# Expert weights in pairs of places, router logits with tokens on partitions, and a later second gather

## The chip, the cores and the metric

One core of a Trainium2 chip runs the whole program. The metric is device time in microseconds (us) of one execution; the number given for a kernel is the median of its runs. A span is the time from the first to the last instruction of a profiled execution.

## The reference

A batch of one sequence of 256 tokens with 1024 features passes a first transformer block and then two layers of a second block; everything is float32. A layer of the second block is

```python
h = h + hybrid_mixer(rmsnorm_2(h, norm_mix[l]), ...)       # two attentions, gates, output projection
h = h + expert_choice_ffn(rmsnorm_2(h, norm_ffn[l]), ...)
```

and the expert part is

```python
cap = CAPACITY_FACTOR * S // N_EXPERTS                      # 2 * 256 / 16 = 32 tokens for each expert
aff = softmax(einsum('bsd,de->bse', h, w_router), axis=-1)  # 256 tokens x 16 experts
gate, idx = top_k(swapaxes(aff, 1, 2), cap)                 # each expert picks its 32 tokens
xe = h[bidx, idx]
a = einsum('becd,edf->becf', xe, w_gate)
u = einsum('becd,edf->becf', xe, w_up)
ye = einsum('becf,efd->becd', silu(a) * u, w_down)
out = zeros_like(h).at[bidx, idx].add(gate[..., None] * ye)
```

All 16 experts run with three matrices of 1024 x 1024 each, so a layer reads 192 MB of expert weights.

## The kernel before

**Program.** `first_block()` runs once; then, for each of two layers, `mixer` and `experts`. The order of the instructions on each engine is chosen by a scheduler that simulates a timeline: of the instructions that are ready it takes the one that stands first in the source. On the chip every engine keeps that order.

**Weights of the experts.** They are stored as 192 chunks a layer (`NCHUNK`), each 128 partitions of 2048 floats: 1 MB in rows of 8 KB. `Experts.load` brings the next chunk to the next place of a fixed cycle: one place "q" (the tile Qb), NA0 = 4 places "a0", NA = 6 places "a1", "Ha" and "Hb" (the two halves of the activations' pair), NB = 1 place "b", RING = 3 places "r" (the ring that also holds the mixer's weights), NSPLIT = 4 places "s" (the buffers of the split mixer weights). The first time round two places "x" follow (parts of W, and XB). That is 21 places, and 23 for the first round. A chunk's DMA is issued on SP's queue and waits there until its place is free. Each DMA also has one of eight semaphores in turn, so a ninth is issued when the first of eight has landed.

**Loading ahead.** While the mixer runs, `prefetch` and `pace` issue the first chunks behind the mixer's own loads: "q" and four "a0" between the query projections, six "a1" between the gate projections (`pace`), "Ha" and "Hb" at the sixth merge, then "b" when the gates' pool closes. The places "r" and "s" come free one by one as the output projection ends, W when the last merged activations M are used up, XB when the tokens' features xg have been transposed (L1133).

**End of the mixer.** The output projection makes eight tiles (`out_tiles`), each of 24 matmuls (L141 to L143) on split weights. After tile k, DVE adds it to x and forms xg[k] = x[k] * gain (L979, L980); ACT squares x[k]. For k = 7 the order is another: xg[7] is finished first (L983, L984), then x[7] (L985), then its square (L987). The router's logits are summed by matmuls with the router's 32 padded columns of feature block k as weights and xg[k], 256 tokens, as moving columns (L994): experts on partitions, four blocks side by side in four groups of 32 partitions; half of them after tile 3, half after tile 7. Then ACT copies the sums (L999), and two matmuls with a constant "sum4" (L1009) add the four groups and turn the result to tokens on partitions. In between, the mean square is summed (L1003) and its root taken by ACT (L201). The logits are scaled by 1/rms (L1014), their maximum is taken off (L1101, L1102), and ACT makes the exponentials (L1103), for which it loads another table.

**Experts.** Each of the four groups of four experts takes 16 chunks for the gate matrices (bank G), 16 for up (U), 16 for down (E), a chunk for eight matmul instructions (L1190). The inputs of the experts are gathered by `gather(k0)`: matmuls with a selection matrix (L1205) and a copy by ACT (L1209), feature block by feature block. `grouped` calls the gather of the next block through `ahead` before the matmuls of each chunk:

```python
for k0 in range(0, KT, kn):
    for b in banks:
        w = xl.take()
        if ahead:
            ahead(k0 + 1)
```

So gather(0) and gather(1) come before the first chunk's matmuls. In the first group the scheduler puts chunks of U between those of G where a gather is waited for. The last 16 chunks of a layer are issued one behind the other, and the last of all as two halves of 4 KB rows.

Of the kernel before, what the change touches and what calls it, by code (L numbers as in the profile page):

```python
# [10 lines left out]
F32 = mybir.dt.float32  # L11
# [27 lines left out]
PV, NPV = _places([("final_g", 8), ("norm_mix", 16), ("b_gate", 32), ("norm_ffn", 16), ("router", 512)])  # L39
# [5 lines left out]
CV, NCV = _places([("ident", 128), ("ones_d", 1), ("ones_h", 1), ("slot", 32), ("sum4", 16)])  # L45
# [8 lines left out]
RING, NA0, NA, NB, NSPLIT = 3, 4, 6, 1, 4  # L54

ENDS = ((0, 512), (512, 256), (768, 256))

SCRATCH = 2048
# [3 lines left out]
def tile_net(ctx: ExitStack, tc: tile.TileContext, a, out):  # L62
# [109 lines left out]
    def act_pair():  # L172
        return tuple(hp.tile([P, KT, T], F32R, name=f"H{c}", tag=f"H{c}") for c in "ab")
# [530 lines left out]
    def mixer(l, h, stats, w0=None):  # L704

        with ExitStack() as es:
# [17 lines left out]
            xl.r2a.append(late.enter_context(tc.tile_pool(name=f"e{l}a0", bufs=NA0, side="right", reuse_waits="tile")))  # L724
# [143 lines left out]
            xl.prefetch(1, True)  # L868
# [51 lines left out]
            xl.r2a.append(late.enter_context(tc.tile_pool(name=f"e{l}a", bufs=NA, side="right", reuse_waits="tile")))  # L920
# [47 lines left out]
            xl.r2b = late.enter_context(tc.tile_pool(name=f"e{l}b", bufs=NB, reuse_waits="tile"))  # L968
            xl.prefetch(NB)
# [3 lines left out]
            at = PV["router"][0] + 256 * l  # L973
# [24 lines left out]
            lp = cp.tile([P, T], F32, name="lp", tag="sq", bufs=2)  # L998
            nc.scalar.copy(lp, pl[:, :T])  # L999
            ms = psv()  # L1000
            for t in range(2):
                for i, s in enumerate((acc, sq7)):
                    nc.tensor.matmul(  # L1003
                        ms[:, t : t + 1], s[:, t * P : t * P + P], con("ones_d"), start=i == 0, stop=i == 1
                    )
# [8 lines left out]
            nc.vector.tensor_tensor(  # L1014
                lg, pls[:, 0:32].rearrange("p (t e) -> p t e", t=2), by_expert(rt), op=ALU.mult
            )
# [7 lines left out]
    class Experts:  # L1024


        def __init__(self, l):
            self.l, self.r2a, self.r2b, self.at, self.dma = l, [], None, 0, None
            self.have, self.n, self.wait = [], 0, 4

            self.cycle = ["q"] + ["a0"] * NA0 + ["a1"] * NA + ["Ha", "Hb"] + ["b"] * NB + ["r"] * RING + ["s"] * NSPLIT
            self.places = self.cycle + ["x", "x"]

        def load(self, paced=False):
            i = len(self.have)
            end = i >= NCHUNK - sum(cn for _, cn in ENDS) * KT // 512
            while True:
                where = self.places.pop(0)
                if not self.places:
                    self.places = list(self.cycle)  # L1040

                if not (end and where in ("Ha", "Hb")):
                    break
# [4 lines left out]
            else:  # L1048
                pool, tag = {
                    "q": (qp, "Qb"), "a0": (self.r2a[0], "w2"), "a1": (self.r2a[-1], "w2"), "b": (self.r2b, "w3"),  # L1050
                    "r": (ring, "w"), "Ha": (hp, "Ha"), "Hb": (hp, "Hb"),
                }[where]
                t = pool.tile([P, CH], F32, name="we", tag=tag)
# [3 lines left out]
            src = a["w_exp"][self.l, i]  # L1057

            for c0, cn in ((0, 1024), (1024, 1024)) if i == NCHUNK - 1 else ((0, CH),):
# [3 lines left out]
            self.have.append(t)  # L1063
# [420 lines left out]
```

## Time and profile before

| | |
|---|---|
| median of 3 runs | 1884.87 us (1884.21 to 1887.2) |
| profiled execution | 1885.2 us, of which span 1883.3 us |
| TensorE busy | 1594.7 us, 85% of the span |
| VectorE busy | 825.0 us, 44% |
| ScalarE busy | 628.9 us, 33% |
| chain that ended last | 53% PE, 44% DMA; 42% DMA of expert weights alone |
| moved by DMA | 562.49 MB, mean 299 GB/s |

The shares are means over stages that differ: in the mixers TensorE is busy all the time and the DMA engines are not, in the experts it is the other way round. The chain that ended last says so in its two large shares.

### The profile page before, as it was taken

Reading aid. Unit: us, or ns where it says so; the run is one execution under the profiler, and the core shown is the slowest. Engines: PE = TensorE matmul, PEld = TensorE weight load, DVE = VectorE, ACT = ScalarE, POOL = GpSimd, SP = SyncE. Lnnn points to the kernel's source line nnn. Section 1 sums busy time; section 2 is a strip of 40 time slices with the busy share of each in tenths; the row PEclk is TensorE's granted clock in tenths of the full one; section 3 lists DMA queues with packets and bytes.
Section 4 is the critical chain, followed back from the end, with each engine's and each line's share of the span. In section 5 each row is a group of like instructions: output and inputs, shape, how many; then the busy total and the mean of one; then the engine's idle time right before and its main releaser. Section 6 shows DMA issues by size and latency. Waiting matters only on the chain.

```text
span 1883.3 us, 27589 instructions
## 1 busy us (share of the span) xinstructions
PE 1594.7 (85%) x11434; PEld 1076.1 (57%) x11434; DVE 825.0 (44%) x1481; ACT 628.9 (33%) x1130; POOL 41.2 (2%) x72
## 2 busy tenths in 40 slices
PE   8999999999999998876777667899998866766765
PEld 7899999999998897220211102888995211101101
DVE  8678777996687666100010001687573110000001
ACT  5566646665566543100000001566542100000001
POOL 0100000000011000000000000010000000000000
PEclk9999999999999999886777767999999877868768
DMA  7454455555562387999999999833487999999997
GB/s 250 169 191 165 171 191 179 179 181 185 217 241 90 114 328 274 402 420 420 419 420 420 420 420 419 340 136 112 181 321 307 419 420 420 419 420 419 420 420 309
DMA packets 83829, 562.49 MB, mean 299 GB/s; under 512 B 9452, under 2 KB 14456, under 8 KB 16888
## 3 DMA queue, kind: packets, MB, share of 16 engines
q1 hardware_dynamic: 83544, 560.20, 75.3%
q8 instruction: 90, 1.47, 0.3%
q10 hardware_dynamic: 160, 0.52, 0.1%
q14 instruction: 35, 0.29, 0.0%
HBM read 558.84 MB, written 1.85 MB: 298 GB/s over the span
## 4 chain that ended last, share of the span: by engine, by line
PE 53%; DMA 44%; DVE 1%; ACT 1%; issue 0%; SPq 0%; POOL 0%; ACTq 0%
DMA we<-in_w_exp_dram 42%; PE ps_d L141 14%; PE ps_d L142 14%; PE ps_d L143 14%; PE ps_t L268 2%; PE ps_v L856 1%; PE ps_g L1190 1%; DMA w<-in_w_in_dram 1%; PE ps_u L1190 1%; PE ps_s L782 1%; PE ps_s L888 1%; PE ps_s L783 1%; PE ps_t L1205 0%; PE ps_s L385 0%; PE ps_v L906 0%; PE ps_v L912 0%
## 5 line engine op out<-in xcount | busy, mean ns | idle before, releaser
L141 PE MATMUL ps_d<-Ha,ws 128*128 128x256 f32 x1408 | 403.6, 287 | 9.4 <-ACT Ha L188 7.7
L143 PE MATMUL ps_d<-Ha,ws 128*128 128x256 f32 x1408 | 403.3, 286 | 1.2 <-DVE ws L136 1.2
L142 PE MATMUL ps_d<-Hb,ws 128*128 128x256 f32 x1408 | 402.4, 286 | 0.2 <-DVE Hb L189 0.2
L136 DVE TENSOR_TENSOR ws<-w,ws 128x1024 fp32r<-128x1024 f32 x282 | 344.3, 1223 | 122.7 <-ACT ws L135 119.6
L135 ACT CAST ws<-w 128x1024 fp32r<-128x1024 f32 x282 | 294.3, 1047 | 277.2 <-PE ps_d L143 248.3
L141 PEld LDWEIGHTS ps_d<-Ha,ws 128*128 128x128 f32 x1408 | 271.9, 193 | 12.7 <-ACT Ha L188 7.7
L143 PEld LDWEIGHTS ps_d<-Ha,ws 128*128 128x128 f32 x1408 | 271.6, 193 | 4.0 <-DVE ws L136 1.8
L142 PEld LDWEIGHTS ps_d<-Hb,ws 128*128 128x128 f32 x1408 | 271.7, 193 | 2.9 <-issue 1.2
L1190 PE MATMUL ps_u<-we,W 128*32 128x512 f32 x992 | 189.0, 840 | 91.5 <-DMA we<-in_w_exp_dram 91.5
L1190 PE MATMUL ps_g<-we,W 128*32 128x512 f32 x1024 | 175.5, 782 | 74.2 <-DMA we<-in_w_exp_dram 74.2
L1190 PE MATMUL ps_e<-we,W 128*32 128x512 f32 (+1 forms) x1152 | 163.2, 671 | 61.7 <-DMA we<-in_w_exp_dram 61.6
L1190 PEld LDWEIGHTS ps_u<-we,W 128*32 128x32 f32 x992 | 25.2, 125 | 241.0 <-DMA we<-in_w_exp_dram 225.8
L1190 PEld LDWEIGHTS ps_g<-we,W 128*32 128x32 f32 x1024 | 26.4, 122 | 208.1 <-DMA we<-in_w_exp_dram 168.9
L1264 ACT ACTIVATE W<-ps_g 128x512 f32<-128x512 f32 x16 | 9.6, 597 | 380.9 <-PE ps_g L1190 380.9
L1190 PEld LDWEIGHTS ps_e<-we,W 128*32 128x32 f32 x1152 | 29.3, 118 | 163.9 <-DMA we<-in_w_exp_dram 124.0
L1266 DVE SCALAR_TENSOR_TENSOR W<-W,ps_u 128x512 f32<-128x512 f32 x16 | 11.0, 688 | 250.9 <-PE ps_u L1190 250.9
L1219 DVE COPY W<-ps_e 128x512 f32<-128x512 f32 (+1 forms) x18 | 11.4, 632 | 220.7 <-PE ps_e L1190 220.7
L1271 ACT COPY W<-ps_t 128x512 f32<-128x512 f32 x16 | 9.4, 586 | 278.4 <-PE ps_t L1270 278.4
L1265 DVE SCALAR_TENSOR_TENSOR W<-W,ps_g 128x512 f32<-128x512 f32 x16 | 11.0, 688 | 208.2 <-ACT W L1264 208.2
L141 PE MATMUL ps_d<-Y,ws 128*128 128x256 f32 x288 | 80.8, 281 | 0.0
L142 PE MATMUL ps_d<-Y,ws 128*128 128x256 f32 x288 | 80.7, 280 | 0.0
L143 PE MATMUL ps_d<-Y,ws 128*128 128x256 f32 x288 | 80.7, 280 | 0.0
(327 smaller groups left out, 2362.6 us busy)
## 6 DMA issues: line engine op xcount, KB each, us to landing
we<-in_w_exp_dram SPq DMA_DIRECT2D x378, 1024.0 KB, 19.9
w<-in_w_in_dram SPq DMA_DIRECT2D x46, 1024.0 KB, 4.9
w<-in_w_up_dram SPq DMA_DIRECT2D x22, 1024.0 KB, 4.8
w<-in_w_br_dram SPq DMA_DIRECT2D x18, 1024.0 KB, 4.8
w<-in_w_gate_dram SPq DMA_DIRECT2D x12, 1024.0 KB, 4.9
w<-in_w_out_dram SPq DMA_DIRECT2D x12, 1024.0 KB, 4.9
w<-in_w_down_dram SPq DMA_DIRECT2D x11, 1024.0 KB, 4.8
w<-in_w_rnn_dram SPq DMA_DIRECT2D x8, 1024.0 KB, 4.8
```

The source lines that it names most:

```text
L135: nc.scalar.copy(ws[:, 0], s)
L136: nc.vector.tensor_tensor(ws[:, 1], s, ws[:, 0].bitcast(F32), op=ALU.subtract)
L141: nc.tensor.matmul(ps, wh, xh, start=first, stop=False)
L142: nc.tensor.matmul(ps, wh, xl, start=False, stop=False)
L143: nc.tensor.matmul(ps, wl, xh, start=False, stop=last)
L268: nc.tensor.transpose(ps[:, i * P : i * P + P], b, ident)
L782: nc.tensor.matmul(ps, q, kh, start=True, stop=False)
L783: nc.tensor.matmul(ps, q, kl, start=False, stop=True)
L856: nc.tensor.matmul(po[64 * c : 64 * c + 64, :T], vw[:, k, kvh * 64 : kvh * 64 + 64], pts[c][:, k * T : k * T + T], start=k == 0, stop=k == 1,)
L888: nc.tensor.matmul(ps[:, o], qa[b, i, tk], ka[b, i, kr], start=True, stop=True)
L1190: nc.tensor.matmul(b[32 * e : 32 * e + 32, :cn], lhs[:, k, 32 * e : 32 * e + 32], cols(w, ((k - k0) * 4 + e) * cn, cn), start=k == 0, stop ...
L1219: nc.vector.tensor_copy(ye[:, s], E[:, :cn])
```

## The change

- Places "a0", "a1", "H" and "b" are joined in pairs: one tile of 128 x 4096 floats, one DMA of 2 MB, the weights packed in the host's array so that a pair has rows of 16 KB. "q", "r", "s", "x" and the last four chunks of a layer stay single. `_plan()` writes the order of places out ahead.
- NB goes from 1 to 2, so the cycle has 22 places and the first round 24. The padding of the router's weights and "sum4" go, and the DMA scratch is halved.
- `prefetch` and `pace` ask half as often for pairs: three times for "q" and "a0" between the query projections instead of five, every second time in `pace`.
- The router's logits are made with xg[k] as weights (128 tokens at a time) and the router's 16 columns as moving operand, two matmuls after each tile; the sum over k is in the accumulation, so L999 and L1009 go. The maximum is taken off before the scaling by 1/rms.
- For k = 7 the order is that of the other tiles: x[7], then xg[7].
- The sums of squares are taken block by block, so that those of `acc` come before those of the last square.
- `ahead` isn't called for the first chunk: gather(1) comes behind the first chunk's matmuls.

```diff
-RING, NA0, NA, NB, NSPLIT = 3, 4, 6, 1, 4
+RING, NA0, NA, NB, NSPLIT = 3, 4, 6, 2, 4
...
+LAST = sum(cn for _, cn in ENDS) * KT // 512
-SCRATCH = 2048
+SCRATCH = 1024
+def _plan():
+    cycle = [("q", 1)] + [("a0", 2)] * (NA0 // 2) + [("a1", 2)] * (NA // 2) + [("H", 2)] + [("b", 2)] * (NB // 2)
+    cycle += [("r", 1)] * RING + [("s", 1)] * NSPLIT
+    places, plan, i = cycle + [("x", 1)] * 2, [], 0
+    while i < NCHUNK:
+        where, n = places.pop(0)
+        places = places or list(cycle)
+        if where == "H" and i + n > NCHUNK - LAST:
+            continue
+        n = n if i < NCHUNK - 4 else 1
+        plan.append((i, n, where))
+        i += n
+    return plan
...
     def act_pair():
-        return tuple(hp.tile([P, KT, T], F32R, name=f"H{c}", tag=f"H{c}") for c in "ab")
+        H = hp.tile([P, 2, KT, T], F32R, name="H", tag="H")
+        return H[:, 0], H[:, 1]
...
                 parts_q(qws[i], load(w1[l, 2 + i]))
-                xl.prefetch(1, True)
+                if i != 2:
+                    xl.prefetch(1, True)
...
             parts_q(qa0, load(w1[l, 6]))
-            xl.prefetch(1, True)
...
-                    xl.prefetch(2, True)
+                    xl.prefetch(1, True)
...
-            xl.prefetch(NB)
+            xl.prefetch(NB // 2)
...
+                    nc.vector.tensor_tensor(x[:, k, :], ps, x[:, k, :], op=ALU.add)
+                    nc.vector.tensor_scalar(xg[:, k, :], x[:, k, :], gain, None, op0=ALU.mult)
                     if k < KT - 1:
-                        nc.vector.tensor_tensor(x[:, k, :], ps, x[:, k, :], op=ALU.add)
-                        nc.vector.tensor_scalar(xg[:, k, :], x[:, k, :], gain, None, op0=ALU.mult)
                         square_in(acc, x[:, k, :], k == 0)
                     else:
-                        nc.vector.tensor_scalar(xg[:, k, :], x[:, k, :], gain, None, op0=ALU.mult)
-                        nc.vector.scalar_tensor_tensor(xg[:, k, :], ps, gain, xg[:, k, :], op0=ALU.mult, op1=ALU.add)
-                        nc.vector.tensor_tensor(x[:, k, :], ps, x[:, k, :], op=ALU.add)
                         sq7 = cp.tile([P, T], F32, name="sq7", tag="sq", bufs=2)
                         nc.scalar.activation(sq7, x[:, k, :], AF.Square)
+                    for t in range(2):
+                        nc.tensor.matmul(
+                            pl[:, 16 * t : 16 * t + 16], xg[:, k, t * P : t * P + P],
+                            pv[:, at + 16 * k : at + 16 * k + 16], start=k + t == 0, stop=k + t == KT,
+                        )
...
-                if j % 2 == 1:
-                    for k in range(2 * j - 2, 2 * j + 2):
-                        o = 32 * (k % 4)
-                        nc.tensor.matmul(
-                            pl[o : o + 32, :T], pv[:, at + 32 * k : at + 32 * k + 32], xg[:, k, :],
-                            start=j == 1, stop=j == 3,
-                        )
-            lp = cp.tile([P, T], F32, name="lp", tag="sq", bufs=2)
-            nc.scalar.copy(lp, pl[:, :T])
...
-            for t in range(2):
-                for i, s in enumerate((acc, sq7)):
+            for i, s in enumerate((acc, sq7)):
+                for t in range(2):
...
-            pls = pss()
-            for t in range(2):
-                nc.tensor.matmul(
-                    pls[:, 16 * t : 16 * t + 16], lp[:, t * P : t * P + P], con("sum4"), start=True, stop=True
-                )
...
+            nc.vector.tensor_reduce(mx, pl, axis=AX.X, op=ALU.max, negate=True)
+            nc.vector.tensor_tensor(lg, pl, by_expert(mx), op=ALU.add)
...
-            src = a["w_exp"][self.l, i]
+            src = a["w_exp"][self.l, i * P * CH : (i + m) * P * CH].rearrange("(p c) -> p c", p=P)
...
-            self.have.append(t)
+            self.have += [t[:, CH * j : CH * j + CH] for j in range(m)]
...
-            self.wait -= 1
-            if self.wait < 0 and len(self.have) < 1 + NA0 + NA:
+            self.asked += 1
+            if self.asked > 4 and self.asked % 2 and len(self.have) < 1 + NA0 + NA:
                 self.load(True)
...
-            nc.vector.tensor_reduce(mx, lg, axis=AX.X, op=ALU.max, negate=True)
-            nc.vector.tensor_tensor(lg, lg, by_expert(mx), op=ALU.add)
+            nc.vector.tensor_tensor(lg, lg, by_expert(rt), op=ALU.mult)
...
-                        if ahead:
+                        if ahead and (k0 > 0 or b is not banks[0]):
                             ahead(k0 + 1)
```

## Rows read from the trace of the kernel before

**Rows 1.** The page's slices of the span (40 of 47 us each), GB/s moved.
```profile
GB/s 250 169 191 165 171 191 179 179 181 185 217 241 90 114 328 274 402 420 420 419 420 420 420 420 419 340 136 112 181 321 307 419 420 420 419 420 419 420 420 309
```

**Rows 2.** Windows: us, busy time of each engine, granted clock, DMA share, GB/s.
```profile
720.00:760.00 40.00, 33.08 (x250) 24.28 (x253) 18.80 (x48) 12.41 (x24) 0.00 (x0) 0.91 0.68 260
...
760.00:1150.00 390.00, 278.09 (x1578) 63.08 (x1570) 27.02 (x44) 16.34 (x35) 0.00 (x0) 0.75 1.01 420
...
1400.00:1420.00 20.00, 20.00 (x159) 18.37 (x157) 12.62 (x25) 7.26 (x11) 0.00 (x0) 1.00 0.73 269
...
1435.30:1444.40 9.10, 6.96 (x40) 3.21 (x40) 2.46 (x6) 0.53 (x2) 0.00 (x0) 0.62 0.13 32
...
1500.00:1850.00 350.00, 236.64 (x1268) 42.32 (x1260) 20.71 (x30) 10.40 (x22) 0.00 (x0) 0.75 1.01 420
```

**Rows 3.** The page's DMA issues: count, size of each, us from issue to landing.
```profile
we<-in_w_exp_dram SPq DMA_DIRECT2D x378, 1024.0 KB, 19.9
w<-in_w_in_dram SPq DMA_DIRECT2D x46, 1024.0 KB, 4.9
```

**Rows 4.** Timeline of PE at the end of layer 0's experts: start, us, instruction.
```profile
1176.04 1.07 PE L1190 MATMUL ps_e<-we,W 128*32 128x256 f32 x16 [1.69 <-DMA we<-in_w_exp_dram]
1178.54 1.07 PE L1190 MATMUL ps_e<-we,W 128*32 128x256 f32 x16 [1.43 <-DMA we<-in_w_exp_dram]
...
1181.08 0.64 PE L1190 MATMUL ps_e<-we,W 128*32 128x256 f32 x8 [0.61 <-DMA we<-in_w_exp_dram]
```

**Rows 5.** Timeline of SP's queue at the end of layer 1's mixer.
```profile
1400.10 25.57 SPq L1062 DMA_DIRECT2D we<-in_w_exp_dram  x8
...
1442.17 7.81 SPq L1062 DMA_DIRECT2D we<-in_w_exp_dram  x7
```

**Rows 6.** Timeline of PE round a group of the router's matmuls in the output projection.
```profile
1411.31 0.28 PE L143 MATMUL ps_d<-M,ws 128*128 128x256 f32 x1
1411.52 0.62 PE L994 MATMUL ps_s<-xg,pv 128*32 128x256 f32 x4
...
1412.30 0.28 PE L142 MATMUL ps_d<-M,ws 128*128 128x256 f32 x1
```

**Rows 7.** Timeline of PE where another dense stream is cut by four small matmuls.
```profile
1193.63 0.28 PE L143 MATMUL ps_d<-Ha,ws 128*128 128x256 f32 x1
1193.75 0.50 PE L195 MATMUL ps_v<-cv,acc 128*128 128x1 f32 x4
...
1194.31 0.28 PE L143 MATMUL ps_d<-ws,Hb 128*128 128x256 f32 x1
```

**Rows 8.** Weight loads of two lines: ns min/median/max of one.
```profile
L994 PEld LDWEIGHTS ps_s<-xg,pv x32: 106/108/109, 723.8 to 1426.2; 128*32 128x32 f32 x32
...
L1003 PEld LDWEIGHTS ps_v<-cv,acc x8: 186/190/192, 738.0 to 1427.1; 128*128 128x128 f32 x8
```

**Rows 9.** Timeline of DVE in the output projection.
```profile
1410.37 1.22 DVE L136 TENSOR_TENSOR ws<-w,ws 128x1024 fp32r<-128x1024 f32 x1
1411.50 0.35 DVE L980 TENSOR_SCALAR xg<-x,pv 128x256 f32<-128x256 f32 x1
```

**Rows 10.** Timeline of DVE, PE and ACT from the last tile to the exponentials.
```profile
1425.36 0.48 DVE L984 SCALAR_TENSOR_TENSOR xg<-ps_d,pv,xg 128x256 f32<-128x256 f32 x1 [1.48 <-PE ps_d L143]
...
1427.42 0.60 PE L1009 MATMUL ps_s<-cv,lp 128*128 128x16 f32 x4
1427.60 0.26 ACT L201 ACTIVATE rtok<-ps_v,eps 128x2 f32<-128x2 f32 x1 [0.40 <-PE ps_v L1003]
...
1427.88 1.28 ACT L1103 ACT_TABLE_LOAD   x1
...
1429.17 0.23 ACT L1103 ACTIVATE lg<-lg 128x32 f32<-128x32 f32 x1
```

**Rows 11.** Timeline of PE at the second gather and the first chunk of layer 1.
```profile
1439.02 1.23 PE L1205 MATMUL ps_t<-sl,ht 128*128 128x128 f32 x4 [0.35 <-ACT W L1209]
...
1440.17 3.08 PE L1190 MATMUL ps_g<-we,W 128*32 128x512 f32 x16
```

More of the change, by code (lines that the diff above doesn't have):

```diff
@@ L723, in mixer @@
             xl = Experts(l)
-            xl.r2a.append(late.enter_context(tc.tile_pool(name=f"e{l}a0", bufs=NA0, side="right", reuse_waits="tile")))
+            xl.r2a.append(late.enter_context(tc.tile_pool(name=f"e{l}a0", bufs=NA0 // 2, side="right", reuse_waits="tile")))
             att = es.enter_context(ExitStack())
@@ L919, in mixer @@
             att.close()
-            xl.r2a.append(late.enter_context(tc.tile_pool(name=f"e{l}a", bufs=NA, side="right", reuse_waits="tile")))
+            xl.r2a.append(late.enter_context(tc.tile_pool(name=f"e{l}a", bufs=NA // 2, side="right", reuse_waits="tile")))
             M = qp.tile([P, 2, KT, T], F32R, name="M", tag="Qa")
@@ L967, in mixer @@
             bp = late.enter_context(tc.tile_pool(name=f"e{l}h", bufs=1, reuse_waits="tile"))
-            xl.r2b = late.enter_context(tc.tile_pool(name=f"e{l}b", bufs=NB, reuse_waits="tile"))
-            xl.prefetch(NB)
+            xl.r2b = late.enter_context(tc.tile_pool(name=f"e{l}b", bufs=NB // 2, reuse_waits="tile"))
+            xl.prefetch(NB // 2)
             acc = new_acc()
             xg = bp.tile([P, KT, T], F32, name="xg", tag="xg")
-            at = PV["router"][0] + 256 * l
+            at = PV["router"][0] + 128 * l
             pl = pss()
@@ L999, in mixer @@
-            nc.scalar.copy(lp, pl[:, :T])
             ms = psv()
-            for t in range(2):
-                for i, s in enumerate((acc, sq7)):
+            for i, s in enumerate((acc, sq7)):
+                for t in range(2):
                     nc.tensor.matmul(
-                        ms[:, t : t + 1], s[:, t * P : t * P + P], con("ones_d"), start=i == 0, stop=i == 1
+                        ms[:, t : t + 1], s[:, t * P : t * P + P], con("ones_d"), start=i + t == 0, stop=i + t == 2
@@ L1028, in __init__ @@
             self.l, self.r2a, self.r2b, self.at, self.dma = l, [], None, 0, None
-            self.have, self.n, self.wait = [], 0, 4
-            self.cycle = ["q"] + ["a0"] * NA0 + ["a1"] * NA + ["Ha", "Hb"] + ["b"] * NB + ["r"] * RING + ["s"] * NSPLIT
-            self.places = self.cycle + ["x", "x"]
+            self.have, self.n, self.plan, self.asked = [], 0, _plan(), 0
         def load(self, paced=False):
[L1035 to L1043, printed above, removed]
+            i, m, where = self.plan.pop(0)
+            end = i >= NCHUNK - LAST
             if where == "x":
@@ L1050, in load @@
                     "q": (qp, "Qb"), "a0": (self.r2a[0], "w2"), "a1": (self.r2a[-1], "w2"), "b": (self.r2b, "w3"),
-                    "r": (ring, "w"), "Ha": (hp, "Ha"), "Hb": (hp, "Hb"),
+                    "r": (ring, "w"), "H": (hp, "H"),
                 }[where]
-                t = pool.tile([P, CH], F32, name="we", tag=tag)
+                size = 2 * CH if where in ("a0", "a1", "H", "b") else CH
+                t = pool.tile([P, size], F32, name="we", tag=tag)
             if paced:
                 nc.gpsimd.tensor_copy(t[:, 0:1], turn[0][:, 0:1].bitcast(F32))
-            src = a["w_exp"][self.l, i]
-            for c0, cn in ((0, 1024), (1024, 1024)) if i == NCHUNK - 1 else ((0, CH),):
+            src = a["w_exp"][self.l, i * P * CH : (i + m) * P * CH].rearrange("(p c) -> p c", p=P)
+            for c0, cn in ((0, 1024), (1024, 1024)) if i == NCHUNK - 1 else ((0, m * CH),):
                 behind = self.dma if end else turn[1] if paced else None
@@ L1097, in bank @@
                 return pp.tile([P, 512], F32, name=f"ps_{tag}", tag=tag, bufs=bufs)
-            mx, sm, m8 = small("rmx", P, 2), small("rsm", P, 2), small("m8", 16, 8)
-            nc.vector.tensor_reduce(mx, lg, axis=AX.X, op=ALU.max, negate=True)
-            nc.vector.tensor_tensor(lg, lg, by_expert(mx), op=ALU.add)
+            sm, m8 = small("rsm", P, 2), small("m8", 16, 8)
+            nc.vector.tensor_tensor(lg, lg, by_expert(rt), op=ALU.mult)
             nc.scalar.activation(lg, lg, AF.Exp)
@@ L1281, in experts @@
                         if not last and c0 + cn == D:
-                            xl.prefetch(NCHUNK - len(xl.have))
+                            xl.prefetch(len(xl.plan))
                             with tc.issue_after(xl.dma.ins):
@@ L1343, in _experts @@
                 chunks.append(w.reshape(4, KT, P, 2, 512).transpose(1, 3, 2, 0, 4).reshape(-1, P, CH))
-    return np.concatenate(chunks, 0)
+    chunks = np.concatenate(chunks, 0)
+    return np.concatenate([chunks[i : i + n].transpose(1, 0, 2).reshape(-1) for i, n, _ in _plan()])
 def _cols(v):
@@ L1361, in _constants @@
     _put(c, CV, "slot", np.broadcast_to(np.arange(1, 33), (P, 32)))
-    _put(c, CV, "sum4", np.tile(np.eye(32, 16), (4, 1)))
     pos = np.arange(T)
@@ L1423, in _pack @@
     put("w_f", fl.reshape(8, P, 8).transpose(1, 0, 2).reshape(P, 64))
-    put("router", np.pad(i["w_router_2"].reshape(2, 8, P, 16).transpose(2, 0, 1, 3), ((0, 0), (0, 0), (0, 0), (0, 16))).reshape(P, 512))
+    put("router", i["w_router_2"].reshape(2, 8, P, 16).transpose(2, 0, 1, 3).reshape(P, 256))
     r["cv"], cmask, oh, r["far"] = _constants()
```

9 lines of the change are left out of this document (4 added, 5 removed).

## The prediction

> **What bounds the kernel now.** I read the slices of the page first. In them the reader is to see two kinds of stage: long stretches at about 420 GB/s, which are the experts of the two layers, and between them stretches at 90 to 330, which are the first block and the mixers [rows 1]. The windows put names to both: in 760 to 1150 and in 1500 to 1850 the DMA engines are busy all the time (share 1.01) while TensorE has about 70% at a mean granted clock of 0.75; in 1400 to 1420, the end of a mixer, TensorE is busy for all of the 20 us and the DMA share is 0.73 [rows 2]. So in the experts a us of TensorE is worth nothing and a MB is worth its transfer; in the mixers it is the reverse. A chunk of 1024 KB at 420 GB/s takes 2.50 us. The issues agree: a chunk lands 19.9 us after its issue, the time of eight, since eight are under way at once, while a mixer's load of the same size, with little in front of it, lands in 4.9, of which 2.5 are transfer and 2.4 lead [rows 3].
>
> Between the two kinds lies the piece that the change is about. SP's queue issues eight chunks from 1400.10 on as places come free, and the next one at 1442.17, when the first chunk has been used [rows 5]. In between all places are full: in 1435.3 to 1444.4 the DMA share is 0.13 [rows 2]. The end of a layer is therefore: the moment when the first chunk is used, 2.4 us of lead, and one transfer after the other for all chunks that were not loaded ahead, 192 less 23. Three things can move it: chunks loaded ahead, the time for a MB, and that moment.
>
> **One more place.** The round before the restart holds 24 chunks in place of 23, if the DMA engines have room for the 24th. They do: it is issued with the other "b" at 1400.10, and 1400 to 1420 leaves them 0.27 of 20 us, 5.4 us; in layer 0, 720 to 760 leaves 0.32 of 40 us [rows 2]. The transfer is hidden there and one fewer stands in the saturated stream: 2.5 us a layer. If the cover were gone, the gain would be nought.
>
> **Rows of 16 KB.** By `_plan()`, 54 pairs, 108 of the 168 chunks behind the first 24, go as pairs. No row of 16 KB is in these rows, so I bound it by the nearest: the last chunk of a layer goes as two halves of 4 KB rows. At the end of layer 0 a chunk in one DMA took 2.50 us, from the first use of the one before it to its own (1176.04 to 1178.54), and the chunk in halves 2.54, to the use of its second half (1178.54 to 1181.08) [rows 4]. So 16 rows for each DMA engine instead of 8, and two DMAs instead of one, cost 0.04 us a MB; going to 4 rows and half a DMA should give back about half of that, 0.02. One reading is good to some 0.02, so the ends are 0 (the time is all in the bytes) and 0.04; I take 0.025: 2.7 us a layer, ends 0 and 4.3. The Trainium skill, "DMA: Bandwidth & Descriptors", section on the iDMA fabric, has a stream of 1 MiB DMAs with 4 KiB rows at 408.7 GB/s. Against the 420 of this trace's 8 KB rows that is, as an estimate from the page, 0.07 us a MB for eight rows and 0.035 for the step to 16 KB, or 3.8 us a layer; no run here yet shows it.
>
> **The moment of the first chunk**, four terms.
>
> (a) Router's matmuls in the dense stream. Before, three groups cut the stream (the fourth comes after the last tile, beside DVE). A cut: from 1411.31 to 1412.30 is 0.99 us, where two steps take 0.24, so 0.75, times three 2.25 [rows 6]. After, seven cuts of four instructions (a float32 matmul is two here: 32 for the 16 matmuls of L994 [rows 8]) with 128 columns of weights and 16 moving. The nearest row is the cut by four matmuls with 128 columns of weights and one moving: 1193.63 to 1194.31, 0.68 less 0.24, so 0.44 [rows 7]; with 16 moving columns I take 0.48, in all 3.35. The last tile ends 1.1 us later; ends 0.4 (six cuts of 0.44, the seventh beside DVE) and 1.6 (0.55 a cut). That TensorE must load 128 columns for 16 in this form can be read in the rows: a load takes 190 ns where the old one took 108 [rows 8]; the 256 moving columns of the old form are gone in return. The Trainium skill speaks against this edit: "TensorE: Matmul & The Clock Gate", section on LDWEIGHTS, makes the load's time grow with its columns, columns/1.2 ns, so 32 loads of 107 ns against 16 of 27, about 3 us more a layer as an estimate. By it alone the sum would be 4 us less gain for both layers; the rows show a cut of four at 0.44, which holds the loads already.
>
> (b) After the last tile. The piece of DVE that stood in front of x[7] (0.48) goes behind it, so its square starts about 0.4 earlier; one of the sums of squares is then already done. The exponentials start at 1429.17 because the table load, right behind the root, takes 1.28 from 1427.88 [rows 10]. That load stays, so moving the maximum ahead and dropping L999 and L1009 (0.60 of TensorE) gives nothing by itself there; dropping L1009 lets the transposes behind it start earlier. I take 0.45 earlier; ends 0.2 and 0.9.
>
> (c) gather(1) behind the first chunk: 1440.17 less 1439.02, 1.15 earlier [rows 11].
>
> (d) What is late next. After the first chunk's place, the next to come free are a pair, which needs two more chunks with gather(1) in front of them, or a single place of a U chunk. gather(1) at 1.15 and two chunks at 0.9 (the first two took 3.08 together at the lower clock [rows 11]) make 2.95, and the first transfer lasts 2.5: 0.5 us of hole; ends 0 and 2.
>
> Together +1.1 - 0.45 - 1.15 + 0.5 = 0.0 a layer; ends -1.2 and +2.
>
> **What I cost at nothing.** Pairs ahead of the mixer's own loads: a load issued behind one lands up to 2.5 us later than behind a single, about 4.9 + 5.0. It is hidden by the ring and the split halves: a load feeds 48 matmuls of 0.12, 5.8 us, and three loads and four halves stand ahead of TensorE, which never waits in 1400 to 1420 [rows 2]. Without that cover each of the six pairs that are loaded ahead there could cost 2.5. On SP's queue the wait for a pair's second place holds up the singles behind it; in the stream eight DMAs are under way, so nothing runs dry. POOL's small copies in front of paced loads are fewer. The end of a layer stays: the last three chunks go as before.
>
> **Sum.** 2 x (2.5 + 2.7 - 0.0) = 10.4 us. The profiled execution took 1885.2, which gives 1874.8; the median of the runs is 0.3 below that execution, so I predict 1874.5.
>
> **Rivals.**
> 1. *Rows of 16 KB give nothing*: the engines are busy all the time before [rows 2], so only a cost for each row can go, and 0.04 is near the error of its reading [rows 4]. Then 2 x 2.5 is left: 1880.2. Chance 0.14.
> 2. *Slower: TensorE waits for xg[k].* It keeps the scheduler's order, and the new matmuls stand in the dense stream soon after their tile, where DVE may be in a split of 1.22 us; xg[2] started at 1411.50 just behind one [rows 9]. At a full split for each, 14 x 1.2 = 17 us are lost: 1892. From a mean wait of 0.74 the gain is gone. Against it: the old cuts stood where xg was ready. Chance 0.10.
> 3. *Late restart*: the hole in (d) at 2 us and the cuts at 0.55, +2 a layer: 1878.8. Chance 0.08.
> 4. *More*: 0.04 for the rows and 1.2 earlier: 2 x (2.5 + 4.3 + 1.2) = 16, 1869. The Trainium skill's section on the iDMA fabric, above, leans this way. Chance 0.10.
>
> **Chances and range.** My forecast has the remaining 0.58; by itself it reaches from 1871 to 1879. The range goes from rival 4 to beyond rival 1, 1867.5 to 1882.5, and leaves out rival 2 and the far tails. A measurement here tells apart about 0.2%, 3.8 us. Faster by more: nearly all of the forecast and of rivals 3 and 4, and two thirds of rival 1, 0.79. Within: the rest of these and the mild waits of rival 2, 0.12. Slower: 0.09.
>
> **What would show it.** The stream's windows should rise from 420 to about 423 or 424 GB/s; if they stay, rival 1. The last chunk that is loaded ahead should land at the same time as before, with 24 in. The first chunk's matmuls should come straight behind the first copy of L1209, and the next issue of SP within half a us of now. In the dense stream the cuts should be 0.45 to 0.5 with no idle of TensorE that ends on DVE's xg; if there is, rival 2. I am wrong if TensorE waits in the mixers for weights, or if SP's order puts a pair's wait ahead of places that are free and the stream has holes.

## The result, and the profile after

The changed kernel took 1868.68 us (median of 4 runs, 1866.66 to 1869.48), the kernel before 1884.76 on the same chip (4 runs): a ratio of 0.9912, 95% interval 0.9900 to 0.9925. That is 16.1 us faster, where 10.4 were forecast; 1868.68 lies in the range (1867.5 to 1882.5), near its low end, where rival 4 stood (1869), and below the 1871 to 1879 that the forecast by itself reached. The profiled span went from 1883.3 to 1867.5 us.

The page's slices of the changed kernel, GB/s, answer to [rows 1]: the experts' plateaus stand at 421 to 427 in place of 419 to 420.

```profile
GB/s 249 147 198 161 161 203 180 182 181 181 187 282 92 122 284 338 353 425 426 423 426 424 424 427 423 354 165 109 158 337 304 421 426 426 425 425 425 424 425 320
```

Its windows answer to [rows 2] (us, busy time of PE, PEld, DVE, ACT and POOL, granted clock, DMA share, GB/s). The stream has 425 GB/s with the DMA engines full as before, so the gain there is not idle time that was filled. In 1400 to 1420 TensorE still works for all of the 20 us, with 314 GB/s beside it in place of 269: the pairs ahead and the 24th chunk are hidden.

```profile
720.00:760.00 40.00, 32.52 (x251) 27.24 (x250) 20.47 (x52) 13.23 (x23) 0.00 (x0) 0.87 0.76 284
760.00:1150.00 390.00, 257.42 (x1616) 68.99 (x1618) 26.93 (x43) 16.70 (x36) 0.00 (x0) 0.81 1.01 425
1400.00:1420.00 20.00, 20.00 (x172) 20.00 (x171) 12.10 (x25) 8.01 (x13) 0.00 (x0) 1.00 0.85 314
1500.00:1850.00 350.00, 219.62 (x1296) 49.12 (x1288) 24.10 (x35) 13.42 (x29) 0.00 (x0) 0.81 1.01 425
```

The page's DMA issues answer to [rows 3]: 122 transfers of 2 MB and 134 of 1 MB stand for the 378 of before, and the mixer's own loads land in 4.9 us as before.

```profile
we<-in_w_exp_dram SPq DMA_DIRECT2D x122, 2048.0 KB, 29.5
we<-in_w_exp_dram SPq DMA_DIRECT2D x134, 1024.0 KB, 24.7
w<-in_w_in_dram SPq DMA_DIRECT2D x46, 1024.0 KB, 4.9
```

SP's queue answers to [rows 5]. The reader is to see the hole in it: from the last place that the mixer frees (the issue into W, 0.4 us behind the last tile) to the first re-used one it is 14.59 us (1419.95 to 1434.54); before it was 16.45 (from the issue into W at 1425.72, below, to 1442.17 [rows 5]).

```profile
1419.58 0.33 SPq L1062 DMA_DIRECT2D we<-in_w_exp_dram  x1
1419.95 0.43 SPq L1062 DMA_DIRECT2D W<-in_w_exp_dram  x1
1423.34 0.33 SPq L1062 DMA_DIRECT2D XB<-in_w_exp_dram  x1
1434.54 10.08 SPq L1062 DMA_DIRECT2D we<-in_w_exp_dram  x7
```

To say where the time went I cut both spans at three issues of SP that both kernels have: into W in either layer, and the mixer's load that waits for a split at the end of layer 0's experts (1187.50 before, 1181.11 after). The places to look at are these lines, of before and then of after; layer 1's W of after stands above.

```profile
737.96 0.43 SPq L1062 DMA_DIRECT2D W<-in_w_exp_dram  x1
...
1187.50 0.33 SPq L118 DMA_DIRECT2D w<-in_w_in_dram  x1
...
1425.72 0.43 SPq L1062 DMA_DIRECT2D W<-in_w_exp_dram  x1
```

```profile
740.37 0.43 SPq L1062 DMA_DIRECT2D W<-in_w_exp_dram  x1
...
1181.11 0.33 SPq L137 DMA_DIRECT2D w<-in_w_in_dram  x1
```

| stretch | before, us | after, us | difference |
|---|---|---|---|
| start to layer 0's W | 737.96 | 740.37 | +2.41 |
| layer 0's W to the mixer's load | 449.54 | 440.74 | -8.80 |
| that load to layer 1's W | 238.22 | 238.84 | +0.62 |
| layer 1's W to the end | 457.54 | 447.54 | -10.00 |

So the experts gave 18.8 us, 9.4 a layer where 5.2 were forecast, and 3 us were lost outside them. That raises three questions: which of the terms is larger than predicted, whether one of them is the router, and what was lost in the front.

### The profile page after: what moved, and what is told of

Read it like the earlier page. It is cut to its first block, busy times and chain, and to the rows that moved or that the text cites. A ratio compares the mean times of both kernels' runs of the same rounds, so it can differ in the third digit from the quotient of the medians.

```text
span 1867.5 us, 27365 instructions
## 1 busy us (share of the span) xinstructions
PE 1545.2 (83%) x11458; PEld 1089.8 (58%) x11458; DVE 824.0 (44%) x1479; ACT 627.9 (34%) x1128; POOL 35.3 (2%) x60
## 4 chain that ended last, share of the span: by engine, by line
PE 53%; DMA 44%; DVE 2%; ACT 0%; issue 0%; SPq 0%; POOL 0%; ACTq 0%; DVEq 0%
DMA we<-in_w_exp_dram 43%; PE ps_d L160 14%; PE ps_d L162 14%; PE ps_d L161 14%; PE ps_t L288 2%; PE ps_v L877 1%; PE ps_g L1190 1%; PE ps_s L802 1%; PE ps_s L908 1%; PE ps_u L1190 1%; PE ps_s L803 1%; PE ps_t L1205 0%; PE ps_s L405 0%; PE ps_v L926 0%; PE ps_v L932 0%
## 5 line engine op out<-in xcount | busy, mean ns | idle before, releaser
L160 PE MATMUL ps_d<-H,ws 128*128 128x256 f32 x1408 | 403.6, 287 | 8.9 <-ACT H L208 7.7
L162 PE MATMUL ps_d<-H,ws 128*128 128x256 f32 x1408 | 403.4, 287 | 0.9 <-DVE ws L155 0.8
L161 PE MATMUL ps_d<-H,ws 128*128 128x256 f32 x1408 | 402.2, 286 | 0.3 <-DVE H L209 0.3
L160 PEld LDWEIGHTS ps_d<-H,ws 128*128 128x128 f32 x1408 | 272.0, 193 | 12.3 <-ACT H L208 7.6
L162 PEld LDWEIGHTS ps_d<-H,ws 128*128 128x128 f32 x1408 | 271.9, 193 | 3.6 <-issue 1.5
L161 PEld LDWEIGHTS ps_d<-H,ws 128*128 128x128 f32 x1408 | 272.0, 193 | 2.3 <-issue 0.8
L1190 PE MATMUL ps_u<-we,W 128*32 128x512 f32 x992 | 168.7, 806 | 107.8 <-DMA we<-in_w_exp_dram 107.8
L1190 PE MATMUL ps_g<-we,W 128*32 128x512 f32 x1024 | 159.0, 734 | 74.5 <-DMA we<-in_w_exp_dram 73.8
L1190 PE MATMUL ps_e<-we,W 128*32 128x512 f32 (+1 forms) x1152 | 155.1, 661 | 73.6 <-DMA we<-in_w_exp_dram 73.6
L1190 PEld LDWEIGHTS ps_u<-we,W 128*32 128x32 f32 x992 | 30.6, 129 | 236.3 <-DMA we<-in_w_exp_dram 185.0
L1190 PEld LDWEIGHTS ps_e<-we,W 128*32 128x32 f32 x1152 | 33.1, 121 | 173.9 <-DMA we<-in_w_exp_dram 125.8
```

The source lines that it names most:

```text
L160: nc.tensor.matmul(ps, wh, xh, start=first, stop=False)
L161: nc.tensor.matmul(ps, wh, xl, start=False, stop=False)
L162: nc.tensor.matmul(ps, wl, xh, start=False, stop=last)
L1190: nc.tensor.matmul(b[32 * e : 32 * e + 32, :cn], lhs[:, k, 32 * e : 32 * e + 32], cols(w, ((k - k0) * 4 + e) * cn, cn), start=k == 0, stop ...
```

## The experiments

The first four ran on one chip with the kernel before at 1885.13 us (median of 10 runs). Their medians carry a scatter of the first block that is explained below, so the verdicts go by stretches of the profiles. The changed kernel's profile on that same chip is f1: 440.10 us from layer 0's W to the mixer's load, 448.83 from layer 1's W to the end. How far two profiles of one kernel differ in these stretches is told with the table of terms below.

**Rows or transfers?** e1 keeps the pairs' places and their single transfers of 2 MB, but each partition reads two rows of 8 KB; e2 gives each pair two transfers of 1 MB.

```diff
-src = a["w_exp"][self.l, i*P*CH : (i+m)*P*CH].rearrange("(p c) -> p c", p=P)
+src = a["w_exp"][self.l, i*P*CH : (i+m)*P*CH].rearrange("(m p c) -> p m c", p=P, m=m)
...
# e1
+nc.sync.dma_start(t[...].rearrange("p (m c) -> p m c", m=m), src)
# e2
+for j in range(m): nc.sync.dma_start(t[:, CH*j : CH*j + CH], src[:, j])
```

> The changed kernel with one edit: the weights of a pair lie as two chunks, so that the same DMA of 2 MB reads two rows of 8 KB for each partition. Number of DMAs, places and order stay. If the length of a row is what made the stream faster (425 GB/s against 420, about 5 us a layer), the stream falls back to 420 and the time rises by about 10 us, to 1879. If fewer and larger DMAs did it, the stream stays at 425 and the time at 1868.7. If my term for the rows (0.025 us a MB) was right and the rest of the gain came from elsewhere, it rises by 5.4, to 1874.

> The changed kernel, pairs of places as they are, but each pair is loaded by two DMAs of 1 MB with 8 KB rows, so eight DMAs under way hold 8 MB again. If the length of a row alone counts: 420 GB/s and 1879, as with one DMA of two rows. [...] If only the number of DMAs counts, 1879 here and 1868.7 in the run with one DMA of two rows.

e1 took 1880.08 us (6 runs, ratio 0.9969, 0.9957 to 0.9981), e2 1876.78 (4 runs, 0.9961, 0.9946 to 0.9976). The windows of e1, then of e2, in the two dense stretches:

```profile
760.00:1140.00 380.00, 252.11 (x1588) 66.69 (x1586) 25.84 (x42) 15.80 (x35) 0.00 (x0) 0.80 1.01 419
1500.00:1840.00 340.00, 212.31 (x1248) 47.59 (x1244) 20.70 (x30) 10.40 (x22) 0.00 (x0) 0.82 1.01 421
```

```profile
760.00:1140.00 380.00, 266.52 (x1571) 63.19 (x1569) 26.25 (x42) 16.12 (x35) 0.00 (x0) 0.78 1.01 420
1500.00:1840.00 340.00, 226.41 (x1220) 42.35 (x1212) 20.72 (x30) 10.40 (x22) 0.00 (x0) 0.76 1.01 421
```

Both are back at 420. With rows of 8 KB one transfer of 2 MB is no better than two of 1 MB; it is the row's length that makes most of the step to 425. In stretches, e1 is 4.37 and 3.06 us longer than f1 (444.47 and 451.89): the rows are worth 7.4 us for both layers together, between the 10 of the first theory and the 5.4 of the third. e2 is 4.40 and 2.35 longer (444.50 and 451.18), 6.8 together. Counted from the DMA packets of each trace between 780 and 1140 us, the stream has 419.7 GB/s before, 420.7 in e1, 420.5 in e2 and 425.0 in the changed kernel. So about 1 of the 5 GB/s is not the rows'; no run here shows what it is.

**The place.** e3 has a single b in place of the pair, so 23 chunks ahead as before the change.

```diff
-RING, NA0, NA, NB, NSPLIT = 3, 4, 6, 2, 4
+RING, NA0, NA, NB, NSPLIT = 3, 4, 6, 1, 4
...
-... + [("b", 2)] * (NB // 2)
+... + [("b", 1)]
...
```

> The changed kernel with a single place b: 23 chunks ahead in place of 24, all else as it is. If the extra chunk goes into idle time of the DMA engines and is one less in the saturated stream, the time rises by one transfer a layer, 2.47 at 425 GB/s, together 4.9 us, to 1873.6. If the gap had no room for it or the stream ends elsewhere, it stays at 1868.7.

It took 1877.42 us (5 runs, ratio 0.996, 0.9946 to 0.9974), and its stretches are 4.31 and 3.07 us longer than f1's, 7.4 where 4.9 were expected. But it has 106 pairs where the changed kernel has 122, so it undoes two things; g3 and g4 below part them.

**The gather.** e4 asks for gather(1) in front of the first chunk again.

```diff
-if ahead and (k0 > 0 or b is not banks[0]):
+if ahead:
```

> The changed kernel with gather(1) in front of the first chunk's matmuls again. By my sum the first chunk's place comes free 1.15 us later but the hole behind its transfer (about 1 us in the trace) closes: a net loss of 0 to 0.6 us a layer, 1868.7 to 1870. If the earlier place counts in full and the hole is nothing, 2.3 us more in all, 1871.

It took 1873.61 us (4 runs, 1869.07 to 1877.52; ratio 0.994, 0.992 to 0.996); its stretches are 2.66 and 1.07 us longer than f1's, 3.7 together, more than either theory allowed. SP's queue in layer 1 shows where: from W to the first re-used place it is 15.75 us, 1.16 more than in the changed kernel.

```profile
1425.83 0.43 SPq L1062 DMA_DIRECT2D W<-in_w_exp_dram  x1
...
1441.58 2.27 SPq L1062 DMA_DIRECT2D we<-in_w_exp_dram  x2
```

The windows of the 20 us that begin 10 us behind layer 1's last tile agree: the changed kernel (first fence) moves 280 GB/s in them, e4 249. The 31 GB/s over 20 us are 0.62 MB, 1.5 us of the stream.

```profile
1429.58:1449.58 20.00, 18.61 (x141) 7.50 (x145) 1.74 (x5) 1.28 (x4) 0.00 (x0) 0.83 0.71 280
```

```profile
1435.46:1455.46 20.00, 18.61 (x140) 7.80 (x144) 1.74 (x5) 1.28 (x4) 0.00 (x0) 0.84 0.64 249
```

In layer 0 the bytes don't part the two orders. e4 moves 249 GB/s there (753.87 to 773.87); with the gather behind the first chunk f1 moves 281 (754.50 to 774.50), but the padded kernel f2, which comes next, 249 as well (746.11 to 766.11).

**The first block.** The change touches little there: a small parameter load shrinks by 256 columns, a constant by 16, Ha and Hb are one tile, and the DMA scratch is halved. And yet its profile ends the first block 3.3 us later. f1 is the changed kernel again, on the chip of the four runs above; f2 adds unused columns, so that the load has its old size. One other line differs, against what the expectation says: the DMA scratch goes from 1024 to 256.

```diff
-("norm_ffn", 16), ("router", 256)])
+("norm_ffn", 16), ("router", 256), ("pad", 256)])
...
-SCRATCH = 1024
+SCRATCH = 256
```

> The changed kernel once more, on the chip that runs the next three, as their baseline. Both theories of the first block (the order of the instructions; the clock by chance) expect 1866 to 1870 us and, in the first block, a TensorE that stands idle for some 2.7 us between 50 and 60 us. If the granted clock between 60 and 70 us decides the scatter of the changed kernel and its variants (0.83 or 0.52 in the five profiles so far), this profile shows one of the two, and the first block ends 3 us later than in the kernel before with 0.83 and 6 us later with 0.52.

> The changed kernel with 256 unused columns added to the first small parameter load, so that it has the size of before; nothing else differs in the source. The theory that the smaller load changes the order that is laid out for the first block, and that this order costs the 3.3 us which the changed kernel loses between 35 and 75 us: TensorE is busy for at least 9.6 of the 10 us between 50 and 60 us, the clock between 60 and 70 us is 1.00, and the time is 3 to 4 us under the changed kernel's on this chip (about 1865). The rival, that the 3.3 us come from the transfers of the first block by chance: the idle time is there again, and the time is within 1 us of the changed kernel's.

f1 took 1871.96 us (4 runs, 1866.46 to 1875.55), f2 1867.96 (4 runs, 1867.05 to 1869.70). The windows at 50 to 60 and 60 to 70 us tell why, first of the changed kernel's first profile, then of f1, then of f2 (the granted clock is the third number from the end):

```profile
50.00:60.00 10.00, 7.27 (x63) 6.94 (x59) 1.68 (x3) 2.93 (x3) 0.96 (x2) 1.00 0.47 153
60.00:70.00 10.00, 9.68 (x51) 8.32 (x52) 9.63 (x21) 4.78 (x17) 2.90 (x5) 0.83 0.65 227
```

```profile
50.00:60.00 10.00, 7.79 (x65) 7.42 (x65) 1.95 (x4) 3.46 (x4) 0.82 (x2) 1.00 0.42 147
60.00:70.00 10.00, 9.53 (x36) 8.48 (x37) 8.87 (x17) 3.66 (x12) 2.93 (x5) 0.50 0.69 246
```

```profile
50.00:60.00 10.00, 9.82 (x74) 9.25 (x75) 4.88 (x8) 2.84 (x4) 2.40 (x4) 1.00 0.52 187
60.00:70.00 10.00, 10.00 (x71) 8.43 (x69) 9.49 (x22) 6.26 (x20) 3.68 (x5) 1.00 0.55 188
```

In the changed kernel TensorE stands idle for 2 to 3 us, and behind it the granted clock is 0.83 in one execution and 0.50, the lower of its two levels (1.2 GHz), for the whole 10 us in the other. In the padded one neither happens. The other profiles agree. In all eight with the small load TensorE has one wait of 2.4 to 3.1 us there, and the clock of 60 to 70 us is 1.00 once, 0.83 four times and 0.50 to 0.52 three times; in all six with the old size the longest wait is 0.6 us and the clock 1.00. The timeline of the changed kernel says what it waits for:

```profile
59.04 1.23 POOL L442 TENSOR_TENSOR cm<-cm,p 128x256 f32<-128x256 f32 x2 [58.60 <-DMA cm<-nck_d]
59.71 0.56 DVE L445 SCALAR_TENSOR_TENSOR z<-ps_s,cm 128x384 f32<-128x384 f32 x1 [6.68 <-POOL cm L442]
...
60.33 1.23 PE L405 MATMUL ps_s<-Qa 64*128 64x256 f32 x4 [3.06 <-DVE z L445]
```

A small result goes out to memory (nck_d) and comes back as cm. SP's queue issues the two steps here first in the changed kernel, then in the padded one (its later profile, g2):

```profile
49.91 0.34 SPq L373 DMA_DIRECT2D nck_d<-nck  x1
52.79 1.93 SPq L436 DMA_DIRECT2D cm<-nck_d  x4
```

```profile
47.72 0.34 SPq L373 DMA_DIRECT2D nck_d<-nck  x1
51.72 2.39 SPq L436 DMA_DIRECT2D cm<-nck_d  x4
```

In the padded kernel the result is 2.2 us earlier out and 1.1 earlier back. The code of the block is the same in both; what differs is the order in which its instructions were laid out on the engines. On VectorE and ScalarE the first 128 us have one order in all kernels with the small load and another in all with the old size, before among them. The DMA scratch is an unlikely cause, though no run changes it alone: the old order stands with 2048 (before), 256 (f2) and 128 (f3), the new one with 1024. Why the layout turns on the load's size is not shown here.

**The router.** f3 is f2 with the router of before (experts on partitions, two bundles, copy, summing product, scale before maximum; the diff is shortened).

```diff
-for t in range(2): matmul(pl[:, 16*t : 16*t+16], xg[:, k, t*P : t*P+P], pv[...16 columns])
+if j % 2 == 1: for k in range(2*j-2, 2*j+2): matmul(pl[o : o+32, :T], pv[...32 columns], xg[:, k, :])
+lp = copy(pl); matmul(pls, lp, con("sum4"))
```

> The kernel with the padded load, but with the router of before: the product with experts on partitions in two bundles of four, the scaled last tile, the copy, the summing product and the order of scale and maximum. Compare with the padded kernel. The prediction's terms give +1.1 us a layer for the cuts and -0.45 us for the chain behind the last tile: without the cuts' lower end, 0.0 to 0.7 us a layer gained by the old router, so 0 to 1.4 us faster than the padded kernel. With six cuts of 0.44 us that lie in the dense stream the two terms cancel, and it is within 0.5 us. The rival, that the new chain behind the last tile is worth more than was predicted (the last tile to the first re-used place's issue went from 16.8 to 15.0 us): 2 to 3 us slower.

f3 took 1867.51 us (4 runs, 1867.03 to 1870.58), f2 1867.96: no difference. SP's queue of f2, then of f3, shows the two halves that cancel. From the first of the eight places to W it is 25.24 us in f2 and 24.80 in f3, so the new cuts cost 0.44; from W to the first re-used place 14.59 and 15.29, so the new chain saves 0.70 (0.28 in layer 0).

```profile
1392.02 25.20 SPq L1062 DMA_DIRECT2D we<-in_w_exp_dram  x8
1417.26 0.43 SPq L1062 DMA_DIRECT2D W<-in_w_exp_dram  x1
...
1431.85 4.25 SPq L1062 DMA_DIRECT2D we<-in_w_exp_dram  x3
```

```profile
1391.68 24.75 SPq L1073 DMA_DIRECT2D we<-in_w_exp_dram  x8
1416.48 0.43 SPq L1073 DMA_DIRECT2D W<-in_w_exp_dram  x1
...
1431.77 4.21 SPq L1073 DMA_DIRECT2D we<-in_w_exp_dram  x3
```

**Rows of 4 KB.** f4 is the changed kernel with all expert transfers in rows of 4 KB.

```diff
+src = a["w_exp"][...].rearrange("(h p c) -> p h c", p=P, h=2 * m)   # c is 1024
+nc.sync.dma_start(t[...].rearrange("p (h c) -> p h c", c=1024), src)
```

> The changed kernel with every expert transfer made of rows of 4 KB instead of 16 or 8 KB; the same bytes, places and transfers. If each row has a fixed price, the 0.048 us per MB between 8 KB and 16 KB doubles on the way to 4 KB: 2.50 + 0.096 = 2.59 us per MB, 404 GB/s in the dense stretches instead of 425, and with 167 MB a layer some 20 us a layer more than the changed kernel: about 1908 us. The rival, that only rows longer than 8 KB gain and shorter ones lose nothing (the two transfers on a queue overlap): 420 GB/s and 1876 to 1880 us.

It took 1900.00 us (4 runs, ratio 1.0078, 1.0052 to 1.0103). Its windows:

```profile
760.00:1140.00 380.00, 245.89 (x1531) 64.04 (x1529) 25.55 (x41) 15.53 (x34) 0.00 (x0) 0.82 1.03 409
1500.00:1830.00 330.00, 204.65 (x1200) 47.09 (x1200) 19.75 (x29) 10.35 (x23) 0.00 (x0) 0.81 1.03 409
```

The rival (nothing lost below 8 KB) falls. A MB takes 2.564 us at 409 GB/s, 2.493 at e1's and e2's 420.6 and 2.467 at 425, where 108 of the 168 streamed chunks are paired. From 4 to 8 KB, 128 rows fewer in a MB save 0.071 us; from 8 to 16 KB, 64 rows fewer save 0.026 x 168/108 = 0.041. That is 0.55 and 0.64 ns for a row: a price for each row, near enough the same at both steps. My 404 GB/s and 1908 us went too far, because I had doubled a 0.048 that is 0.041 at most.

**The place again, and what the padding is worth.** g1 and g2 are the changed and the padded kernel on another chip; g3 is the padded one with b as two places of one chunk, g4 with one, both with 106 pairs.

```diff
# g3
-... + [("b", 2)] * (NB // 2)
+... + [("b", 1)] * NB
# g4, besides
-RING, NA0, NA, NB, NSPLIT = 3, 4, 6, 2, 4
+RING, NA0, NA, NB, NSPLIT = 3, 4, 6, 1, 4
```

> The changed kernel, timed in five rounds beside the padded one. Two theories of what the first block's lost time is worth: from the profiles, the block ends 3 us later with a clock of 0.83 between 60 and 70 us and 6 us later with 0.5, so that the runs scatter by 3 us and more and the padded kernel is 3 to 6 us faster by the medians (this one 1869 to 1873). The rival, from the lowest runs so far (1866.5 and 1866.7 here, 1867.05 padded): in some runs the loss is not there at all, and the medians are within 2 us.

> The changed kernel with the 256 unused columns again, timed in five rounds: 1866 to 1868 us with a scatter of under 3 us by the first theory (the first block's idle time and its fall of the clock are gone in every run); by the rival the same scatter as the changed kernel's.

> The padded kernel with the pair b as two places of one chunk: 24 chunks ahead as before it, but 8 pairs a layer fewer (106 transfers of 2 MB in place of 122). Against the padded kernel only rows change: 16 MB a layer at 0.037 to 0.045 us, 0.6 to 0.7 us a layer slower, 1.2 to 1.5 in all. Against the next one, which has one b and the same number of pairs, only the place changes. The theory that a place is worth one transfer: 2.5 us a layer faster than the next, 5 in all. The rival, that the place is worth more (3.1 to 3.4 a layer, from the 3.7 to 4.0 read for the single b less its lost pairs): 6 to 7 us faster.

> The padded kernel with a single b, so 23 chunks ahead, and the same number of pairs as the one before. 5 us slower than that one if a place is worth one transfer of 2.5 us a layer, 6 to 7 if it is worth more; 6.3 to 8 slower than the padded kernel.

g1 1870.28 us (6 runs, 1868.45 to 1875.32), g2 1868.17 (4 runs, 1867.54 to 1869.15), g3 1869.26 (4 runs, 1867.36 to 1869.86), g4 1874.18 (4 runs, 1873.72 to 1875.22); before 1884.66. The place, g4 less g3, is 4.9 us by the medians and 6.3 by the two profiled spans (1871.9 and 1865.6): 2.5 to 3.2 us a layer. One transfer accounts for the median; whether the place is worth somewhat more is not settled. The 16 lost pairs, g3 less g2, are 1.1 us by the medians.

The windows of g1 show a third form of the first block: TensorE idle for 2.4 us, and a clock that stays at 1.00.

```profile
50.00:60.00 10.00, 7.60 (x64) 7.27 (x61) 2.31 (x4) 2.97 (x3) 1.23 (x2) 1.00 0.49 170
60.00:70.00 10.00, 10.00 (x69) 8.90 (x68) 9.72 (x22) 6.21 (x20) 2.60 (x4) 1.00 0.65 216
```

At the load that is issued at 133.27 us in the kernel before, g1 is 1.2 us later, the first profile (0.83) 3.3 and f1 (0.50) 6.3. So the idle time by itself costs about 1 us, and the fall of the clock, which follows it in some executions, 2 to 5 more. The times agree: of 14 executions of the changed kernel four took 1875.1 to 1875.6 us and ten 1866.5 to 1870.4; of 8 padded ones none is above 1869.7. The median of the 14 is 1869.6, of the 8 padded 1868.2: padded, it beats both kernels in the median, by 1.4 us over the changed one (by 4.0 on the chip of f1 and f2, by 2.1 on that of g1 and g2); on the latter the ratios to before are 0.9913 (0.9900 to 0.9926) and 0.9931 (0.9919 to 0.9942), whose intervals overlap. Both theories of g1 had a part of it: in most executions the loss is small, and in a few it is larger. That the four of 1875 us are those with a clock of 0.50 is not shown for each: one of them was profiled (f1). The kernel before, which has no such wait, ranges as far on the chip of f1, from 1882.53 to 1891.42.

## Why the prediction came out as it did

The mechanism was right: the experts' stream is bound by the DMA engines, and the end of a layer moves with the chunks ahead, the time for a MB and the moment of the first chunk. The direction and the range held; the sum was short by a third. What came is rival 4, which had a chance of 0.10: more for the rows and an earlier restart. That the range held is owed to its low end, which was set by that rival. The reasons follow. The terms, in us for both layers:

| term | predicted | measured | by |
|---|---|---|---|
| rows of 16 KB | 5.4 | 7.4 | e1 against f1 |
| one more place | 5.0 | 4.9 to 6.3 | g4 against g3 |
| gather(1) and the hole, (c) and (d) | 1.3 | 3.7 | e4 against f1 |
| router, (a) and (b) | -1.3 | 0.1 | f3 against f2 |
| first block | 0 | -1.4 (medians) | 14 runs against 8 |
| sum | 10.4 | 14.7 to 16.1 | whole change: 16.1 |

Entries from a pair of profiles are good to about 1 us. The experts of the changed and the padded kernel are the same, and their five profiles (the first, f1, g1; f2, g2) have 888.3 to 890.3 us in the two stretches of the experts together. Against these e1 is 6.0 to 8.1 longer and e4 2.3 to 4.4, where f1 alone gives 7.4 and 3.7.

**Rows of 16 KB**: the step that failed is "going to 4 rows and half a DMA should give back about half of that, 0.02". The halving was right, the 0.04 it started from was not: it was read from one chunk at the end of a layer [rows 4], and over whole stretches 4 KB rows cost 0.071 us a MB more than 8 KB rows (f4). Half of that is 0.035, which is what e1 measures: 7.4 us over 216 paired MB are 0.034. The rates of the stream give 0.041 (above); all three are over the 0.025 that I took. The Trainium skill, "DMA: Bandwidth & Descriptors", section on the iDMA fabric, gives 408.7 GB/s for 1 MiB transfers in 4 KiB rows; f4 shows 409. The estimate from that page stood in the prediction, 3.8 us a layer; measured are 3.7. Where the page's figure and a single short reading differed, the run sides with the page. Rival 1 falls.

**One more place**: right, the 24th chunk is hidden (the last chunk ahead lands at 1432.09 by the trace, 2.4 us ahead of the restart), and a transfer a layer is gained. My sign that it lands at the same time as before failed: behind the issue into W it lands 12.14 us later, where the 23rd landed 9.51 later, one transfer more; the hole has room for it.

**(c) and (d)**: gather(1) was costed at 1.15; the stretch from W to the first re-used place is 1.16 us longer in e4's layer 1 (15.75 against 14.59 in the changed kernel) and 0.82 in layer 0, so rival 3, a late restart, falls. The term that was wrong is the hole of 0.5. I costed it for the new order alone and not for the old one. SP's second issue does come later, 3.4 us behind the first where it was 1.15, so my sign "within half a us of now" failed. But the first transfer lands 3.62 us ahead of the second before (1446.93 and 1450.55), and 3.5 us lie between them after in layer 0 (759.81 and 763.33), so nothing was added. With (d) at nought the term is 2.3, or 2.0 by e4's two restarts. The rest of the 3.7 lies in layer 0, whose stretch is 442.76 us in e4, 2.66 longer than in f1 for a restart 0.82 later. But f2, with the gather behind the first chunk, has 442.09 there. So the size of this term is known to 2 to 4 us, and what lengthens layer 0 in some profiles is open.

**(a)**: six cuts of 0.44 stand in the dense stream and the seventh behind the last tile: the lower end that I gave. The changed kernel's timeline shows one; by the measure used for [rows 7], 1412.62 to 1413.31 is 0.69, less 0.24.

```profile
1412.62 0.28 PE L162 MATMUL ps_d<-M,ws 128*128 128x256 f32 x1
1412.75 0.52 PE L1006 MATMUL ps_s<-pv,xg 128*128 128x16 f32 x4
...
1413.31 0.28 PE L161 MATMUL ps_d<-M,ws 128*128 128x256 f32 x1
```

So (a) is +0.4 and not +1.1; moving 16 columns in place of one adds nothing that these rows show. The estimate of some 3 us a layer more that spoke against the edit, from the Trainium skill, "TensorE: Matmul & The Clock Gate", section on LDWEIGHTS, counted the loads alone, without the 256 moving columns that go in return; f3 against f2 shows 0.44. The rule itself, a load's time by its columns, is not refuted by that: by the same section of the Trainium skill four loads of 128 columns take, as an estimate, 0.43 us, and the cut above is 0.45 with its four loads. **Rival 2** falls: TensorE's only idle time that ends on xg is 0.20 us, at the last tile. **(b)** is 0.3 to 0.7, in the ends given. As predicted, the table load sets the exponentials; in the changed kernel it still follows the root at once:

```profile
1420.45 0.62 PE L1006 MATMUL ps_s<-pv,xg 128*128 128x16 f32 x4
...
1421.54 0.26 ACT L221 ACTIVATE rtok<-ps_v,eps 128x2 f32<-128x2 f32 x1 [1.02 <-PE ps_v L1016]
...
1421.82 1.28 ACT L1102 ACT_TABLE_LOAD   x1
...
1423.12 0.23 ACT L1102 ACTIVATE lg<-lg 128x32 f32<-128x32 f32 x1
```

**What I did not see**: the first block. The prediction had no term for a parameter load that shrinks by 256 columns, not even under what it costs at nothing, and the order that comes with it costs 1.2 to 6.3 us in a profile. Beside the 0.4 us of (a) it is the loss of the change, and the padded kernel has it back. The profile that was compared also gained 1.3 us by chance: between 510 and 515 us the granted clock was 0.66 in the kernel before and 1.00 in the changed one. The padded kernel shows both in one program: 1.00 in f2, 0.70 in g2, and g2 takes 1.4 us longer from the load of the first block (133.27 before) to layer 0's W (605.19 against 603.77). With 16.1 from the terms without the first block, 3.3 lost there and these 1.3, 14.1 of that profile's 15.8 are explained. The 1.7 left are about what separates two profiles of one kernel (f1's stretch from layer 1's W to the end is 1.3 longer than that of the first profile); the 1 GB/s that is not the rows' (e1 and e2) would be worth 1.8 over the 336 streamed MB.

## What to carry to other kernels

In a stretch where the DMA engines are full, make the rows longer before anything else: halving the number of rows was worth 0.034 to 0.071 us a MB here, and one transfer of 2 MB at rows of 8 KB was no better than two of 1 MB. Take such a price from whole stretches, not from the last transfer of one, and when a moved step seems to open a hole, look whether the old order had the same hole. Where a scheduler lays out the order, compare the profile of a block that the change should not touch as well; a few unused columns moved it by 1 to 6 us.

## What the runs showed of the hardware that was not expected

The same idle time of TensorE, 2.2 to 2.7 us between 50 and 60 us, is followed by a granted clock of 1.00, 0.83 or 0.50 in the next 10 us, in three executions of one program. So a short wait has a price of its own (1.2 us at the end of the first block) and a chance of a larger one (3.3 and 6.3). The 14 times of the kernel with this wait fall in two groups, 5 us apart, and the 8 of the padded one in one. With so few of them that alone could be chance; the profiles of the first block are the firmer sign.
